# Expert routing: the weight blocks' low halves go from GpSimd to VectorE, a third pair of weight tiles, one staging copy per four tokens

## The chip, the cores and the metric

One core of one Trainium2 chip runs the whole kernel. The metric is the device time of one execution in microseconds, of which a lower one is better; the time shown is the median of several executions of the compiled program. One further execution is recorded by the hardware profiler, and all rows below come from it.

## The reference

The kernel computes two network blocks on 512 tokens of width 1024, all in fp32. The change lies in the first block, in its layer of product-key experts (PEER). Cut to what matters here:

```python
PEER_HEADS, PEER_NKEYS, PEER_TOPK = 8, 128, 16        # 128 x 128 experts
def block(xb):                                        # xb: 128 tokens x 1024
    q = (xb @ w_query).reshape(T, PEER_HEADS, 2, PEER_HALF)
    s = jnp.einsum('thpk,hpnk->thpn', q, sub_keys)
    top_s, top_i = lax.top_k(s, PEER_TOPK)
    cand_s = top_s[:, :, 0, :, None] + top_s[:, :, 1, None, :]
    cand_i = top_i[:, :, 0, :, None] * PEER_NKEYS + top_i[:, :, 1, None, :]
    best_s, best_pos = lax.top_k(cand_s.reshape(...), PEER_TOPK)
    idx = jnp.take_along_axis(cand_i.reshape(...), best_pos, axis=-1)
    gate = jax.nn.softmax(best_s, axis=-1)
    act = jax.nn.gelu(jnp.einsum('td,thkd->thk', xb, expert_u[idx]), approximate=False)
    return jnp.einsum('thk,thkd->td', gate * act, expert_v[idx])
```

Each token uses 8 x 16 = 128 of 16384 experts.

## The kernel before

The 512 tokens are four groups of 128. Group 0 is done sparsely: for each of its 128 slots an indirect DMA on GpSimd's queue gathers one row of `u` per token (later one of `v`), and VectorE takes the dot product with `hT0` (L712). This is the generator `sparse`; `y0["ahead"]` says how many gathers are issued ahead of the dot product that uses them. Groups 1 to 3 (384 tokens) are done densely: TensorE multiplies the tokens with all 16384 rows of `u`, in 128 blocks of 128 experts, and a matrix `Wd` of gates (expert by token, zero where an expert wasn't chosen) masks the result.

Every fp32 weight tile is used as two halves: `whi`, a cast to the matmul's fp32r made by ScalarE, and `wlo`, the difference, made by the engine in `lo_eng[0]` (`split`, L261 to L263). A block (`ublock`, L663) is 24 products of 128x384 in eight k-steps of three, followed by a Gelu on ScalarE into `ge`, which is stored to `gd` in HBM. 76 (`AHEAD`) of the 128 blocks are done during the routing, between other work, and the rest in the loop over experts behind it, whose first product writes `py` (L1002).

The routing runs as follows.

- `gemm_cm("w_q", ...)` with `cons_q` (L735) makes the queries and scores. ScalarE copies the query tile to `qc` (L737), and VectorE finds the 16 best keys of each half (the last row of that is L748).
- `route(t)` (L783) makes, for group t, the 16 best of the candidates, their indices (`eq`, L814, a comparison of 128x800) and the gates, on VectorE. For t = 0 that ends in `idx0`, which the gathers need. For t > 0 `pk` (gates and the two index halves, last cast L836) is transposed on TensorE (L841) and copied to `pT`. `route` yields seven times inside its heads and then a few times more.
- `scatter(t)` (L850) builds `Wd` for group t. Per token it needs a one-hot `ao` (128x128, row index times gate) and a one-hot `bo`, whose product on TensorE (L879) is the token's 128x128 gate matrix. VectorE makes four tokens' `bo` in one operation (L856) and most `ao` (L868), ScalarE makes some `ao` in two steps (`ab` L865, `ao` L866). ScalarE copies the products, four tokens at a time, to `stg` (L881). A scatter yields 16 times, each time after 8 tokens.
- The driver (L891) calls `lookahead(nb, ns)` at each yield: `nb` blocks (or half a block in a scatter), some stores of `Wd`, and `ns` steps of the sparse group. It runs route 0, route 1, scatter 1, route 2, scatter 2, route 3, scatter 3, and then the blocks that are left up to 76.

`lookahead` keeps five raw tiles loading ahead (`us`, `uload`) and splits the next two blocks (`usplit`). The raw tiles and the gather targets come from rings set by `set_ring`, the halves from the pool `whl` with two buffers each. Before, the routing runs with:

```python
        lo_eng[0] = G
            y0 = {"ahead": 5}
            gemm_cm("w_q", range(16), 8, ah, al, cons_q, cols=128, late=LATE[1])
                        if w == 3 and u % 8 == 0:
        lo_eng[0] = V
```

so that GpSimd makes every `wlo` from the query product to the end of the routing. The order of instructions on each engine is decided by a scheduler at build time from the program's order and its dependencies, and each engine runs its own row in that order.

Of the kernel before, what the change touches and what calls it, by code (L numbers as in the profile page):

```python
# [8 lines left out]
F32 = mybir.dt.float32  # L9
F32R = mybir.dt.float32r  # L10
# [171 lines left out]
def build(tc, A, out):  # L182
    nc = tc.nc
    V, S, G, PE = nc.vector, nc.scalar, nc.gpsimd, nc.tensor
    with ExitStack() as ctx:
# [5 lines left out]
        def rpool(name, bufs=1):  # L191
            return pool(name, bufs, side="right")
# [17 lines left out]
        whl = body.enter_context(pool("whl", 2))  # L210
# [13 lines left out]
        def set_ring(w=2048, **n):  # L224

            rawx.close()
            ring.update(w=w, i={}, n={}, p={})
            grow_ring(**n)
# [36 lines left out]
        lo_eng = [G]  # L265
# [42 lines left out]
        def gemm_cm(*a, **k):  # L308
            for _ in gemm_gen(*a, **k):
                pass  # L310
# [132 lines left out]
        with rpool("hg") as hg:  # L443
# [15 lines left out]
            with rpool("hgl") as hl_:  # L459
                lmask = hl_.tile([128, 7, 128], F32)  # L460
                nc.scalar.dma_start(lmask, A["cst"][:, 3:])
                q = hl_.tile([128, 4, T], F32)
# [156 lines left out]
        rawx.close()  # L619
        gp = peer.enter_context(pool("gp"))  # L620
        AHEAD = 76
        set_ring(1024, raw=6, g=5)
        set_banks(pg=2, ps=6)
        hT0 = gp.tile([128, D], F32)
        gate0 = gp.tile([128, 128], F32)
# [23 lines left out]
        Wd = dr.tile([128, 128, ND], F32)  # L649
        gd = dr.tile([AHEAD, 128, ND], F32)  # L650

        def uload(b):
            raw = rawtile((8, 128))
            nc.sync.dma_start(raw.rearrange("p k c -> p (k c)"), A["uT"][b])
            return raw

        def usplit(raw):
            hi = whl.tile([128, 8, 128], F32R, name="whi")
            lo = whl.tile([128, 8, 128], F32R, name="wlo")
            split(raw, hi, lo, lo_eng[0])  # L660
            return hi, lo

# [63 lines left out]
        lo_eng[0] = G  # L726
        with ExitStack() as rt0, ExitStack() as rt_:
            rt = rt0.enter_context(rpool("rt"))
            rk = rt_.enter_context(rpool("rk"))
            keys = rk.tile([128, 16, 128], F32)  # L730
            nc.sync.dma_start(keys, A["keysT"])
# [15 lines left out]
                    V.max(ts[t][:, n, 8:], s2)  # L747
                    V.max_index(ti[t][:, n, 8:], ts[t][:, n, 8:], s2)  # L748

            y0 = {"ahead": 5}  # L750

            rest = sparse(y0)
            nu = [0, 0.0]
            pend = []
# [23 lines left out]
                    nu[1] -= 1  # L778

            gemm_cm("w_q", range(16), 8, ah, al, cons_q, cols=128, late=LATE[1])  # L780
            rt_.close()
            rs = rt_.enter_context(rpool("rs"))

            def route(t):
# [49 lines left out]
                V.tensor_scalar(ii[:, 1], ii[:, 0], 127, None, op0=OP.bitwise_and)  # L834
                V.tensor_scalar(ii[:, 0], ii[:, 0], 7, None, op0=OP.logical_shift_right)
                V.tensor_copy(pk[:, 1:3], ii)  # L836
                yield
                yield
                pp = psum()
                for a in range(3):  # L840
                    PE.transpose(pp[:, a * 128:(a + 1) * 128], pk[:, a], ident)  # L841
# [7 lines left out]
            def scatter(t):  # L849

                pT, nT = tr[t]
                stg = [rs.tile([128, 32, 128], F32, name=f"stg{q}") for q in range(4)]

                def onehots(u):
                    bo = rs.tile([128, 4, 128], F32, name="bo", bufs=3)
                    V.tensor_tensor(bo, iota[:, None, :].to_broadcast([128, 4, 128]),  # L856
                                    pT[:, 1, u:u + 4, None].to_broadcast([128, 4, 128]), op=OP.is_equal)
                    aos = []
                    for w in range(4):
                        tk = u + w  # L860
                        ao = rs.tile([128, 128], F32, name="ao", bufs=8)
                        if w == 3 and u % 8 == 0:

                            ab = rt.tile([128, 128], F32, name="ab", bufs=2)
                            S.activation(ab, iota, AF.Abs, bias=nT[:, 1, tk:tk + 1])  # L865
                            S.activation(ao, ab, AF.Relu, scale=nT[:, 0, tk:tk + 1], bias=pT[:, 0, tk:tk + 1])  # L866
                        else:
                            V.tensor_scalar(ao, iota, pT[:, 2, tk:tk + 1], pT[:, 0, tk:tk + 1], op0=OP.is_equal, op1=OP.mult)  # L868
                        aos.append(ao)
                    return bo, aos  # L870

                oh = [onehots(0)]
                for u in range(0, 128, 4):
                    if u < 124:
                        oh.append(onehots(u + 4))
                    bo, aos = oh.pop(0)
                    pw = psum()
                    for w in range(4):
                        PE.matmul(pw[:, w * 128:(w + 1) * 128], aos[w], bo[:, w], start=True, stop=True)  # L879
                    for q in range(4):  # L880
                        S.copy(stg[q][:, :, u:u + 4].rearrange("p i t -> p t i"),  # L881
                               pw.rearrange("p (t i) -> p t i", t=4)[:, :, q * 32:(q + 1) * 32])
                    if u % 8 == 4:
                        yield
                for q in range(4):
                    for i in range(0, 32, 4):
                        pend.append((Wd[q * 32 + i:q * 32 + i + 4, :, t * 128 - 128:t * 128].rearrange("i p t -> p i t"),
                                     stg[q][:, i:i + 4]))

            tr = {}  # L890
            for t in range(2):  # L891
# [12 lines left out]
            for _ in range(y0["ahead"] - 1):  # L904
                y0["ahead"] -= 1
                next(rest)
        lo_eng[0] = V

        yx = peer.enter_context(rpool("yx"))
        dg = yx.tile([128, 4, 128], F32)  # L910
# [51 lines left out]
        with rpool("ex") as ex:  # L962
# [45 lines left out]
            w = (256 - y0["i"]) / (AHEAD + (LAST - AHEAD) * 3)  # L1008
# [39 lines left out]
            for n in range(2):  # L1048
                raw = rawtile((8, 128))
                nc.sync.dma_start(raw, A["w_in2"][0].rearrange("p (k c) -> p k c", k=8)[:, :, n * 128:n * 128 + 128])  # L1050
                first[n] = whalf(raw, 8, 0, 128)
            q = finish([1, 2, 3], py)
# [418 lines left out]
        with rpool("sd") as sd:  # L1471
# [25 lines left out]
            u = d32("u")  # L1497
# [217 lines left out]
        for d in range(2):  # L1715
            pos_ = [psum("po") for _ in range(4)]
            for j in range(4):
                raw = rawtile((2, 512))
                nc.sync.dma_start(raw.rearrange("p k c -> p (k c)"), A["w_out2"][d * 4 + j])
                hi = whl.tile([128, 2, 512], F32R, name="whi")  # L1720
                lo = whl.tile([128, 2, 512], F32R, name="wlo")
# [27 lines left out]
        ahead = {}  # L1749
# [31 lines left out]
        q = rsqrt(vv, 4)  # L1781
# [213 lines left out]
        for p in range(16):  # L1995
            o, q = divmod(p, 2)
# [108 lines left out]
```

## Time and profile before

| what | value |
|---|---|
| time, median of 3 executions | 3310.78 us (3307.57 to 3311.12) |
| the profiled execution's own time | 3308.83 us |
| its span in the trace | 3307.1 us |
| mean granted clock of TensorE | 0.977 |
| TensorE busy | 3110.3 us, 94% |
| VectorE busy | 2199.8 us, 67% |
| ScalarE busy | 1122.1 us, 34% |
| GpSimd busy | 816.2 us, 25% |
| `wlo` on GpSimd (L263), whole kernel | 120 operations, 306.6 us |
| `wlo` on VectorE (L263), whole kernel | 190 operations, 220.2 us |

Busy time is the time in which an instruction of that engine runs; a matmul's end is modelled, and an instruction of VectorE that is held up inside counts as busy. The span leaves out what lies around the recorded work, here 1.7 us. PE is TensorE, DVE VectorE, ACT ScalarE, POOL GpSimd, SP the queue that issues plain DMAs.

### The profile page before, as it was taken

Reading aid. Unit: us, or ns where it says so; the run is one execution under the profiler, and the core shown is the slowest. Engines: PE = TensorE matmul, PEld = TensorE weight load, DVE = VectorE, ACT = ScalarE, POOL = GpSimd, SP = SyncE. Lnnn points to the kernel's source line nnn. Section 1 sums busy time; section 2 is a strip of 40 time slices with the busy share of each in tenths; the row PEclk is TensorE's granted clock in tenths of the full one; section 3 lists DMA queues with packets and bytes.
Section 4 is the critical chain, followed back from the end, with each engine's and each line's share of the span. In section 5 each row is a group of like instructions: output and inputs, shape, how many; then the busy total and the mean of one; then the engine's idle time right before and its main releaser. Section 6 shows DMA issues by size and latency. Waiting matters only on the chain. (4 is left out here: it accounts for less than half of the span.)

```text
span 3307.1 us, 54224 instructions
## 1 busy us (share of the span) xinstructions
PE 3110.3 (94%) x21581; PEld 2423.5 (73%) x21581; DVE 2199.8 (67%) x4329; ACT 1122.1 (34%) x2012; POOL 816.2 (25%) x495
## 2 busy tenths in 40 slices
PE   7999996878999999999989999999999988999997
PEld 4877786878988888999977777777777756444443
DVE  5834689997828887888976767676568763232323
ACT  3222332645633333333333323332265532111111
POOL 2221244354344444555510000000001151000000
PEclk9999998989999999999999999999999988999999
DMA  5243335375599999999932222222364346899995
GB/s 201 73 182 115 134 104 163 122 245 181 168 345 375 369 368 328 353 358 359 355 109 103 71 73 75 75 75 69 102 248 155 131 154 242 366 403 403 394 412 222
DMA packets 234707, 725.85 MB, mean 219 GB/s; under 512 B 21904, under 2 KB 110736, under 8 KB 197456
## 3 DMA queue, kind: packets, MB, share of 16 engines
q1 hardware_dynamic: 187312, 567.64, 46.5%
q0 software_dynamic: 36864, 134.23, 11.2%
q10 hardware_dynamic: 10272, 20.45, 1.7%
q8 instruction: 171, 2.80, 0.3%
q14 instruction: 88, 0.72, 0.1%
HBM read 658.93 MB, written 63.31 MB: 218 GB/s over the span
## 5 line engine op out<-in xcount | busy, mean ns | idle before, releaser
L262 ACT CAST whi<-raw 128x1024 fp32r<-128x1024 f32 (+1 forms) x310 | 310.8, 1003 | 715.6 <-PE pg L292 384.2
L263 POOL TENSOR_TENSOR wlo<-raw,whi 128x1024 fp32r<-128x1024 f32 x120 | 306.6, 2557 | 550.9 <-ACT whi L262 475.0
L291 PE MATMUL pg<-ah,whi 128*128 128x512 f32 x1056 | 427.3, 405 | 3.5 <-DVE th L1435 2.8
L292 PE MATMUL pg<-al,whi 128*128 128x512 f32 x1056 | 424.2, 402 | 1.7 <-DVE al L263 1.7
L293 PE MATMUL pg<-ah,wlo 128*128 128x512 f32 x1056 | 422.7, 401 | 1.7 <-POOL wlo L263 1.6
L670 PE MATMUL pg<-ah,wlo 128*128 128x384 f32 x1024 | 349.6, 341 | 37.9 <-POOL wlo L263 34.5
L670 PE MATMUL pg<-ah,whi 128*128 128x384 f32 x1024 | 352.9, 345 | 2.3 <-ACT ge L672 1.8
L670 PE MATMUL pg<-al,whi 128*128 128x384 f32 x1024 | 348.0, 340 | 0.0
L263 DVE TENSOR_TENSOR wlo<-raw,whi 128x1024 fp32r<-128x1024 f32 (+1 forms) x190 | 220.2, 1160 | 190.1 <-ACT whi L262 187.2
L1002 PE MATMUL py<-vh,gh 128*128 128x512 f32 x768 | 299.5, 390 | 2.3 <-ACT ge L672 2.3
L1004 PE MATMUL py<-vh,gl 128*128 128x512 f32 x768 | 300.6, 391 | 0.0
L1003 PE MATMUL py<-vl,gh 128*128 128x512 f32 x768 | 300.4, 391 | 0.0
L700 POOL DMA_INDIRECT g<-in_u_dram,idx x128 | 196.2, 1533 | 268.1 <-DVE g L712 221.1
L291 PEld LDWEIGHTS pg<-ah,whi 128*128 128x128 f32 x1056 | 199.9, 189 | 52.1 <-issue 5.9
L293 PEld LDWEIGHTS pg<-ah,wlo 128*128 128x128 f32 x1056 | 200.2, 190 | 46.8 <-POOL wlo L263 2.4
L292 PEld LDWEIGHTS pg<-al,whi 128*128 128x128 f32 x1056 | 200.2, 190 | 44.4 <-issue 3.6
L670 PEld LDWEIGHTS pg<-ah,wlo 128*128 128x128 f32 x1024 | 196.7, 192 | 41.7 <-POOL wlo L263 38.0
L700 POOL DMA_INDIRECT g<-in_v_dram,idx x128 | 189.0, 1477 | 135.5 <-DVE y L720 100.4
L670 PEld LDWEIGHTS pg<-ah,whi 128*128 128x128 f32 x1024 | 196.8, 192 | 4.9 <-ACT ge L672 2.1
L1894 PE MATMUL pf<-we,XT 128*64 128x512 f32 x720 | 197.9, 596 | 2.3 <-ACT XT L1980 2.3
L670 PEld LDWEIGHTS pg<-al,whi 128*128 128x128 f32 x1024 | 196.4, 192 | 2.1
L1946 DVE TENSOR_TENSOR mrg<-mrg,pc 128x512 f32<-128x512 f32 x128 | 84.5, 684 | 139.7 <-PE pc L1944 139.7
(658 smaller groups left out, 6010.3 us busy)
## 6 DMA issues: line engine op xcount, KB each, us to landing
raw<-in_uT_dram SPq DMA_DIRECT2D x128, 512.0 KB
raw<-in_v_dram SPq DMA_DIRECT2D x128, 512.0 KB
raw<-in_w_in_dram SPq DMA_DIRECT2D x54, 1024.0 KB
we<-in_we_down_dram SPq DMA_DIRECT2D x47, 1024.0 KB
we<-in_we_up_dram SPq DMA_DIRECT2D x46, 1024.0 KB
we<-in_we_gate_dram SPq DMA_DIRECT2D x44, 1024.0 KB
araw<-in_w_ada_dram SPq DMA_DIRECT2D x24, 1024.0 KB
Wd<-stg SPq DMA_DIRECT2D x96, 256.0 KB
```

Source lines behind the costliest of these rows:

```text
L262: S.copy(dst_hi, src)
L263: (eng or V).tensor_sub(dst_lo, src, dst_hi.bitcast(F32))
L291: a = PE.matmul(ps, l_ix(lh, k), r_ix(rh, k), start=k == 0, stop=False)
L292: a = PE.matmul(ps, l_ix(lh, k), r_ix(rl, k), start=False, stop=False)
L293: a = PE.matmul(ps, l_ix(ll, k), r_ix(rh, k), start=False, stop=k == kc - 1)
L670: PE.matmul(ps[:, :ND], w[:, k], a[:, k, 128:], start=k + n == 0, stop=k + n == 9)
L700: G.indirect_dma_start(out=raw, out_offset=None, in_=u if i < 128 else v, in_offset=bass.IndirectOffsetOnAxis(ap=idx0[:, k:k + 1], axis=0))
L1002: PE.matmul(py[t][d], gh[:, tk], vh[:, dsl], start=b == 0, stop=False)
L1003: PE.matmul(py[t][d], gh[:, tk], vl[:, dsl], start=False, stop=False)
L1004: PE.matmul(py[t][d], gl[:, tk], vh[:, dsl], start=False, stop=b == 127)
L1894: PE.matmul(pp[e * CAP:(e + 1) * CAP], xg(hf * 4 + k, e), ws[e][k], start=hf + k == 0, stop=hf == 1 and k == 3)
L1946: V.tensor_add(xo, xo, po)
```

## The change

From the end of the query product on, VectorE makes `wlo` instead of GpSimd, whose queue then holds only the gathers. A third pair of `whi` and `wlo` tiles, in the pool `whx`, is used by every third block while the routing lasts; the raw ring has five tiles instead of six and the gather ring four instead of five, and three gathers are issued ahead instead of five. The staging tile of a scatter is one tile instead of four, written by one copy of 128x512 per four tokens instead of four of 128x128. ScalarE makes the fourth `ao` of every four tokens, instead of every second four. `route(t)` for t > 0 yields three times behind its last cast instead of twice, so that one block more lies in each. After the change the lines are numbered 6 to 10 higher.

```diff
--- before.py
+++ after.py
@@ -619,7 +619,7 @@
         rawx.close()
         gp = peer.enter_context(pool("gp"))
         AHEAD = 76
-        set_ring(1024, raw=6, g=5)
+        set_ring(1024, raw=5, g=4)
         set_banks(pg=2, ps=6)
         hT0 = gp.tile([128, D], F32)
         gate0 = gp.tile([128, 128], F32)
@@ -654,9 +654,16 @@
             nc.sync.dma_start(raw.rearrange("p k c -> p (k c)"), A["uT"][b])
             return raw
 
+        whx = []
+
         def usplit(raw):
-            hi = whl.tile([128, 8, 128], F32R, name="whi")
-            lo = whl.tile([128, 8, 128], F32R, name="wlo")
+            p = whl
+            if whx:
+
+                p = whx[0] if whx[1] % 3 == 2 else whl
+                whx[1] += 1
+            hi = p.tile([128, 8, 128], F32R, name="whi")
+            lo = p.tile([128, 8, 128], F32R, name="wlo")
             split(raw, hi, lo, lo_eng[0])
             return hi, lo
 
@@ -726,6 +733,7 @@
         lo_eng[0] = G
         with ExitStack() as rt0, ExitStack() as rt_:
             rt = rt0.enter_context(rpool("rt"))
+            whx += [rt0.enter_context(rpool("whx")), 0]
             rk = rt_.enter_context(rpool("rk"))
             keys = rk.tile([128, 16, 128], F32)
             nc.sync.dma_start(keys, A["keysT"])
@@ -747,7 +755,7 @@
                     V.max(ts[t][:, n, 8:], s2)
                     V.max_index(ti[t][:, n, 8:], ts[t][:, n, 8:], s2)
 
-            y0 = {"ahead": 5}
+            y0 = {"ahead": 3}
 
             rest = sparse(y0)
             nu = [0, 0.0]
@@ -778,6 +786,8 @@
                     nu[1] -= 1
 
             gemm_cm("w_q", range(16), 8, ah, al, cons_q, cols=128, late=LATE[1])
+
+            lo_eng[0] = V
             rt_.close()
             rs = rt_.enter_context(rpool("rs"))
 
@@ -834,8 +844,8 @@
                 V.tensor_scalar(ii[:, 1], ii[:, 0], 127, None, op0=OP.bitwise_and)
                 V.tensor_scalar(ii[:, 0], ii[:, 0], 7, None, op0=OP.logical_shift_right)
                 V.tensor_copy(pk[:, 1:3], ii)
-                yield
-                yield
+                for _ in range(3):
+                    yield
                 pp = psum()
                 for a in range(3):
                     PE.transpose(pp[:, a * 128:(a + 1) * 128], pk[:, a], ident)
@@ -849,7 +859,7 @@
             def scatter(t):
 
                 pT, nT = tr[t]
-                stg = [rs.tile([128, 32, 128], F32, name=f"stg{q}") for q in range(4)]
+                stg = rs.tile([128, 128, 128], F32, name="stg")
 
                 def onehots(u):
                     bo = rs.tile([128, 4, 128], F32, name="bo", bufs=3)
@@ -859,7 +869,7 @@
                     for w in range(4):
                         tk = u + w
                         ao = rs.tile([128, 128], F32, name="ao", bufs=8)
-                        if w == 3 and u % 8 == 0:
+                        if w == 3:
 
                             ab = rt.tile([128, 128], F32, name="ab", bufs=2)
                             S.activation(ab, iota, AF.Abs, bias=nT[:, 1, tk:tk + 1])
@@ -877,15 +887,11 @@
                     pw = psum()
                     for w in range(4):
                         PE.matmul(pw[:, w * 128:(w + 1) * 128], aos[w], bo[:, w], start=True, stop=True)
-                    for q in range(4):
-                        S.copy(stg[q][:, :, u:u + 4].rearrange("p i t -> p t i"),
-                               pw.rearrange("p (t i) -> p t i", t=4)[:, :, q * 32:(q + 1) * 32])
+                    S.copy(stg[:, :, u:u + 4].rearrange("p i t -> p t i"), pw.rearrange("p (t i) -> p t i", t=4))
                     if u % 8 == 4:
                         yield
-                for q in range(4):
-                    for i in range(0, 32, 4):
-                        pend.append((Wd[q * 32 + i:q * 32 + i + 4, :, t * 128 - 128:t * 128].rearrange("i p t -> p i t"),
-                                     stg[q][:, i:i + 4]))
+                for i in range(0, 128, 4):
+                    pend.append((Wd[i:i + 4, :, t * 128 - 128:t * 128].rearrange("i p t -> p i t"), stg[:, i:i + 4]))
 
             tr = {}
             for t in range(2):
@@ -904,7 +910,7 @@
             for _ in range(y0["ahead"] - 1):
                 y0["ahead"] -= 1
                 next(rest)
-        lo_eng[0] = V
+        whx.clear()
 
         yx = peer.enter_context(rpool("yx"))
         dg = yx.tile([128, 4, 128], F32)
```

The first place is VectorE's row in scatter 3, just behind the operation that ends route 3 (`nT`, L845). `bo` and `ao` are the one-hots. Before, they stand there alone:

```order
L845 TENSOR_SCALAR nT<-pT 128x256
L856 TENSOR_TENSOR bo<-cst,pT 128x512
L868 TENSOR_SCALAR ao<-cst,pT 128x128 x3
L856 TENSOR_TENSOR bo<-cst,pT 128x512
L868 TENSOR_SCALAR ao<-cst,pT 128x128 x4
L856 TENSOR_TENSOR bo<-cst,pT 128x512
L868 TENSOR_SCALAR ao<-cst,pT 128x128 x3
L856 TENSOR_TENSOR bo<-cst,pT 128x512
L868 TENSOR_SCALAR ao<-cst,pT 128x128 x4
```

In the changed program the same place reads:

```order
L866 TENSOR_TENSOR bo<-cst,pT 128x512
L878 TENSOR_SCALAR ao<-cst,pT 128x128 x3
L263 TENSOR_TENSOR wlo<-raw_7096,whi 128x1024
L878 TENSOR_SCALAR ao<-cst,pT 128x128 x3
L866 TENSOR_TENSOR bo<-cst,pT 128x512
L878 TENSOR_SCALAR ao<-cst,pT 128x128 x3
L866 TENSOR_TENSOR bo<-cst,pT 128x512
L878 TENSOR_SCALAR ao<-cst,pT 128x128 x3
L866 TENSOR_TENSOR bo<-cst,pT 128x512
L263 TENSOR_TENSOR wlo<-raw_7138,whi 128x1024
L878 TENSOR_SCALAR ao<-cst,pT 128x128 x3
```

There are three `ao` of every four tokens now, and one `wlo` for about every four `bo`.

The second place is GpSimd's row where the routing goes from A to the first scatter; `g` is a gather's target, `idx` holds `idx0`. Before:

```order
L263 TENSOR_TENSOR wlo<-raw_5359,whi 128x1024
L263 TENSOR_TENSOR wlo<-raw_5401,whi 128x1024
L263 TENSOR_TENSOR wlo<-raw_5444,whi 128x1024
L700 DMA g_7680<-in_u_dram,idx_2289 128x1024
L700 DMA g_7911<-in_u_dram,idx_2289 128x1024
L700 DMA g_8130<-in_u_dram,idx_2289 128x1024
L263 TENSOR_TENSOR wlo<-raw_5486,whi 128x1024
L700 DMA g_8209<-in_u_dram,idx_2289 128x1024
L700 DMA g_8288<-in_u_dram,idx_2289 128x1024
```

In the changed program the whole stretch of the routing reads like this:

```order
L707 DMA g_6002<-in_u_dram,idx_2289 128x1024
L707 DMA g_6217<-in_u_dram,idx_2289 128x1024
L707 DMA g_6432<-in_u_dram,idx_2289 128x1024
L707 DMA g_6635<-in_u_dram,idx_2289 128x1024
L707 DMA g_7397<-in_u_dram,idx_2289 128x1024
L707 DMA g_7612<-in_u_dram,idx_2289 128x1024
L707 DMA g_7827<-in_u_dram,idx_2289 128x1024
L707 DMA g_8030<-in_u_dram,idx_2289 128x1024
```

No `wlo` is left between the gathers, so that a gather waits only for `idx0` and a free target.

The third place is ScalarE's row in scatter 3, with the casts (`whi`), the Gelu (`ge`), the copies (`stg`) and the one-hots (`ab`, `ao`). Before:

```order
L881 COPY stg_7205<-ps 128x4x32
L881 COPY stg_7206<-ps 128x4x32
L881 COPY stg_7207<-ps 128x4x32
L881 COPY stg_7208<-ps 128x4x32
L262 CAST whi<-raw_7723 128x1024
L672 ACTIVATE ge<-pg 128x384
L881 COPY stg_7205<-ps 128x4x32
L881 COPY stg_7206<-ps 128x4x32
L881 COPY stg_7207<-ps 128x4x32
L881 COPY stg_7208<-ps 128x4x32
L866 ACTIVATE ao<-ab,pT,nT 128x128
```

In the changed program:

```order
L262 CAST whi<-raw_7542 128x1024
L679 ACTIVATE ge<-pg 128x384
L890 COPY stg<-ps 128x4x128
L876 ACTIVATE ao<-ab,pT,nT 128x128
L890 COPY stg<-ps 128x4x128
L875 ACTIVATE ab<-cst,nT 128x128
L876 ACTIVATE ao<-ab,pT,nT 128x128
L875 ACTIVATE ab<-cst,nT 128x128
L890 COPY stg<-ps 128x4x128
L876 ACTIVATE ao<-ab,pT,nT 128x128
L890 COPY stg<-ps 128x4x128
L876 ACTIVATE ao<-ab,pT,nT 128x128
```

Four copies became one, and between two casts there are now four pairs `ab` and `ao`, not two.

## Rows read from the trace of the kernel before

**Rows 1.** Stretches A to T: us; PE, PEld, DVE, ACT, POOL busy; PEclk, DMA share, GB/s.

```profile
463.20:574.00 110.80, 82.75 (x445) 80.66 (x444) 109.47 (x336) 34.47 (x47) 55.72 (x27) 0.88 0.49 159
574.00:648.50 74.50, 65.59 (x435) 62.88 (x435) 73.96 (x190) 52.76 (x173) 26.36 (x10) 0.97 0.29 91
648.50:717.30 68.80, 47.92 (x258) 46.31 (x257) 68.80 (x146) 18.39 (x30) 42.78 (x22) 0.88 0.94 297
717.30:793.60 76.30, 67.28 (x437) 64.50 (x437) 75.25 (x160) 51.11 (x171) 23.92 (x8) 0.95 0.29 98
793.60:841.50 47.90, 46.13 (x257) 45.48 (x256) 12.71 (x20) 16.73 (x28) 30.70 (x15) 0.96 1.05 335
841.50:905.80 64.30, 62.35 (x437) 61.15 (x437) 63.83 (x142) 49.29 (x170) 20.02 (x8) 1.00 0.35 122
905.80:970.70 64.90, 61.43 (x352) 60.18 (x350) 10.43 (x11) 25.05 (x39) 35.61 (x17) 1.00 1.02 329
```

**Rows 2.** Timeline of GpSimd: start, duration, engine, line, operation, wait before it.

```profile
730.64 2.95 POOL L263 TENSOR_TENSOR wlo<-raw,whi 128x1024 fp32r<-128x1024 f32 x1 [9.39 <-ACT whi L262]
738.39 3.71 POOL L263 TENSOR_TENSOR wlo<-raw,whi 128x1024 fp32r<-128x1024 f32 x1 [4.80 <-ACT whi L262]
...
913.34 2.38 POOL L263 TENSOR_TENSOR wlo<-raw,whi 128x1024 fp32r<-128x1024 f32 x1 [1.78 <-ACT whi L262]
917.50 2.38 POOL L263 TENSOR_TENSOR wlo<-raw,whi 128x1024 fp32r<-128x1024 f32 x1 [1.77 <-ACT whi L262]
```

**Rows 3.** Waits of TensorE from 463.2 to 970.7: total us, times, longest.

```profile
PE pg L670 <- POOL wlo L263: 34.5, 10, 14.0
PE ps L879 <- DVE ao L868: 23.6, 20, 4.4
```

**Rows 4.** Timeline of VectorE in S1; x4 is four operations taken together.

```profile
581.64 1.11 DVE L868 TENSOR_SCALAR ao<-cst,pT 128x128 f32<-128x128 f32 x4
582.67 0.68 DVE L856 TENSOR_TENSOR bo<-cst,pT 128x512 f32<-128x512 f32 x1
583.27 2.94 DVE L868 TENSOR_SCALAR ao<-cst,pT 128x128 f32<-128x128 f32 x3
```

**Rows 5.** Timeline of GpSimd beside it.

```profile
583.67 2.46 POOL L263 TENSOR_TENSOR wlo<-raw,whi 128x1024 fp32r<-128x1024 f32 x1 [6.41 <-ACT whi L262]
```

**Rows 6.** Groups of VectorE in S1, then in R2: count, busy us, mean ns.

```profile
L868 DVE TENSOR_SCALAR ao<-cst,pT 128x128 f32<-128x128 f32 x109 | 45.8, 479 | 0.5 <-PE ps L879 0.5
...
L712 DVE SCALAR_TENSOR_TENSOR g<-g,hT 128x1024 f32<-128x1024 f32 x12 | 24.0, 1997 | 0.0
L814 DVE TENSOR_TENSOR eq<-bpf,cst 128x800 f32<-128x800 f32 x8 | 7.9, 983 | 0.0
L868 DVE TENSOR_SCALAR ao<-cst,pT 128x128 f32<-128x128 f32 x2 | 0.6, 334 | 0.0
```

**Rows 7.** Timeline of VectorE and of GpSimd in S1, around a gather.

```profile
598.56 1.22 DVE L712 SCALAR_TENSOR_TENSOR g<-g,hT 128x1024 f32<-128x1024 f32 x1
...
599.70 0.87 DVE L868 TENSOR_SCALAR ao<-cst,pT 128x128 f32<-128x128 f32 x3
...
600.06 0.95 POOL L700 DMA_INDIRECT g<-in_u_dram,idx  x1 [5.57 <-DVE ao L868]
```

**Rows 8.** A group of VectorE in A.

```profile
L814 DVE TENSOR_TENSOR eq<-bpf,cst 128x800 f32<-128x800 f32 x16 | 23.6, 1476 | 0.0
```

**Rows 9.** Groups of ScalarE in S3: count, busy us, mean ns.

```profile
L881 ACT COPY stg<-ps 128x128 f32<-128x128 f32 x124 | 33.4, 431 | 10.9 <-PE ps L879 10.9
L262 ACT CAST whi<-raw 128x1024 fp32r<-128x1024 f32 x8 | 8.4, 1044 | 4.1 <-issue 4.1
L866 ACT ACTIVATE ao<-ab,pT,nT 128x128 f32<-128x128 f32 x16 | 7.8, 485 | 0.0
```

**Rows 10.** ScalarE's copies `qc` in the query product: shortest/median/longest ns.

```profile
L737 ACT COPY qc<-pg x16: 575/575/581, 369.4 to 464.2; 128x512 f32<-128x512 f32 x16
```

**Rows 11.** Waits of SP's DMA queue from 990 to 1280 us, in the expert loop.

```profile
SPq L968 <- DVE vl L263: 119.9, 61, 3.0
```

## The prediction

> **What bounds the kernel now.** I read the busy table cut at the stages of the routing first, then the waits of TensorE, then the rows of VectorE, GpSimd and ScalarE. The stretch that the change touches runs from 463.2 to 970.7 us. I call its seven pieces, in the order of the rows, A (routing of token groups 0 and 1), S1, R2, S2, R3, S3 (scatter and routing of groups 1 to 3 by turns) and T (the expert blocks left over) [rows 1]. The reader is to see that VectorE is busy throughout A, S1, R2, S2 and S3 and nearly idle in R3 and T. TensorE, which must do 76 blocks of the hidden layer in any case, is not: it idles, and its granted clock has a mean of 0.88 in A and R2, the two pieces where it idles most, so part of them ran at the lower of its levels (1.2 against 2.4 GHz).
>
> How much is lost: a block alone takes 4.16 us (in T the low halves of one block and the next start at 913.34 and 917.50), and in a scatter a block with its 16 one-hot products takes 7.75 us where nothing is late (730.64 to 738.39) [rows 2]. Now 38 blocks lie in A, R2 and R3, 24 in the scatters, 14 in T: 52 x 4.16 + 24 x 7.75 = 402 us. The stretch takes 507.5, so about 105 us are waits and slow clock. Of the waits 34.5 us are for `wlo` from GpSimd, 23.6 us for `ao` from VectorE [rows 3]. The longest of them, 14.0 us, lies in A, where GpSimd's queue holds gathers, which need VectorE's `idx0`, ahead of the next `wlo`.
>
> **Why VectorE is full.** Its busy time is partly waiting. Four `ao` at 581.64 are followed 1.03 us later by a `bo`, and that 0.60 us later by three more `ao` [rows 4]: an `ao` left alone is 0.257 us of VectorE's time, a `bo` 0.60. But those three take 2.94 us, because GpSimd makes a `wlo` from 583.67 on [rows 5]; left alone, three take 0.87 (599.70) [rows 7], so 2.1 us are lost. The mean `ao` of S1 is 479 ns, one left alone 334 ns by itself: 109 x 0.145 = 15.8 us lost to 8 `wlo` [rows 6], and S2 loses about as much. In R2 twelve dot products (L712) average 1997 ns against 1.22 us for the one at 598.56, left alone: 9.3 us [rows 6, 7]. Summed over all groups of R2 in the same way I get 21.4 us. In A the sixteen operations of L814 average 1476 ns where R2 has 983: 7.9 us [rows 6, 8], with the other groups 27. So each `wlo` on GpSimd costs VectorE 1.6 to 2.4 us, and TensorE waits for VectorE.
>
> **The change, part by part.** *The subtraction on VectorE.* The 190 that VectorE makes elsewhere average 1.16 us (the table of the profile before); the dot product of the same size at 598.56 lets the next operation start after 1.14 [rows 7], which I take. It removes the stall of 1.6 to 2.4. GpSimd keeps only gathers, and these do not stall VectorE: at 599.70 three `ao` take 0.87 us with a gather at 600.06 in their middle [rows 7].
>
> *A.* VectorE is busy 109.5 of the 110.8 us [rows 1]. Less 25 of stalls (2 fall into the query product's end), plus 18 `wlo` x 1.14 = 20.5 by the order: 4.5 us less. I take 6, since VectorE no longer starts with work left over from a stalled query product. Its new order has no `wlo` for some 24 us in the middle of A, so TensorE still idles there, and A stays bound by VectorE. 110.8 becomes **104.5**, with one block more done in its idle time (19).
>
> *S1, S2, S3.* A block costs VectorE 4 x 0.60 + 12 x 0.257 + 1.14 = 6.6 us now (four `ao` of 16 go to ScalarE, not two), below TensorE's 7.75; before, 4 x 0.60 + 14 x 0.257 + 2.1 = 8.1, above it. So TensorE binds: 8 x 7.75 = 62, with 1 to 1.5 for the start **63.5, 63.5 and 63** against 74.5, 76.3 and 64.3.
>
> *The copies and `ab`/`ao` on ScalarE.* Sixteen copies a block at 33.4 / 124 = 0.27 us [rows 9] become four of 128x512; such a copy takes 0.575 us for `qc` [rows 10], where the target is contiguous. Bounds: 4 x 0.575 = 2.3 us a block, or no gain, 4.3. I take 2.3: the small copies wrote the same stride. ScalarE is busy 49.3 us for the 8 blocks of S3 [rows 1], 6.2 each; less 2.0, plus two pairs `ab`, `ao` at 0.485 an operation [rows 9], 1.9: 6.1, or 8.1 by the other bound, which is above TensorE's 7.75 by 0.4, 3 us a scatter. By the order each `ao` of ScalarE stands a half-block ahead of its product, so no wait is added.
>
> *R2.* VectorE's 68.8 us lose 21.4 of stalls and seven of the twelve dot products, which the new order puts elsewhere (7 x 1.14 = 8), and gain 12 `wlo` (13.7): 53, less 2 for other rows that moved, 51. VectorE begins it some 3 us before TensorE ends S1, and the first one-hots need 1.5: **49.5**. TensorE's own 11 blocks need 45.8.
>
> *R3.* 11 blocks instead of 10, 45.8 us, and 2 for DMA (rival 1): **48** against 47.9. *T.* 11 blocks instead of 14, 45.8, and 5 for DMA and for the turn to the expert loop: **51** against 64.9.
>
> *Third pair, rings.* A block's `whi` and `wlo` wait for the block three back, not two, so the cast can be done when VectorE comes to its `wlo`: covered. With one raw tile less the load is still issued five blocks ahead. Price if not: one 512 KB load at 335 GB/s [rows 1], 1.6 us, now and then.
>
> *Gathers.* `ahead` 3 and fewer turns of the last loop leave 4 of 256 gathers more to the expert loop: 2.1 MB. There SP waits 119.9 us for VectorE to free raw tiles [rows 11], so DMA runs ahead of use: 0, at most 2.1 MB / 335 GB/s = 6 us if it does not. The loop begins with less loaded, since T is shorter: I take 3 us, bounds 0 and 10.
>
> Sum: 104.5 + 63.5 + 49.5 + 63.5 + 48 + 63 + 51 = 443 against 507.5, -64.5, and +3: **-61.5 us**. From the profiled execution's 3308.8 us that is 3247; its time lies 2 us below the median of the runs, so, rounded, **3250 us**.
>
> **A rule against it.** By the row at 599.70 gathers cost VectorE nothing [rows 7]. The Trainium skill, "SBUF — State Buffer", section "Who interferes with whom", says that VectorE and GpSimd share one pair of ports, which an `ao` in a two-port mode and a gather's descriptors would lock against each other: whichever starts first blocks the other wholly. By the row the sum stays; by the rule each gather in the routes and scatters has a price, and rival 3 is the outcome.
>
> **Rivals.**
> 1. *DMA takes the saving back.* R2, R3 and T ran at 297, 335 and 329 GB/s with the DMA share at 0.94 to 1.05 [rows 1]: 20.4, 16.0 and 21.4 MB. A gather is 0.52 MB, a block 0.72 (load and `gd`). After: R2 seven gathers less, one block more, 17.5 MB; R3 one block and three gathers more, 18.3; T three blocks less, 19.2. At those three rates 59, 55 and 58 us, 9.5 + 7 + 7 = 23 above mine: **3273**. For it: shares at 1. Against it: R3 ran blocks at near their own pace at this load, and stores may end in the next scatter, which uses 91 to 122 GB/s.
> 2. *TensorE binds everywhere but in A:* R2 46, R3 46, T 48, nothing at the loop's start: **3238**.
> 3. *Gathers stall VectorE:* some 12 of them in A and R2, where VectorE binds, each for its own 0.95 us [rows 7]: 11 us, **3261**. The row at 599.70 speaks against it.
> 4. *Slower: VectorE stands in line behind ScalarE.* Now `wlo` waits in VectorE's queue for the cast, the cast behind ScalarE's copies, the copies for TensorE's products, and the next `ao` behind `wlo`. If the one-hots kept ahead (three `bo`, eight `ao`) did not cover that, a scatter block would add copy 0.6 [rows 10], cast 1.04 [rows 9] and `wlo` 1.2 to 7.75: 10.6 us, 85 a scatter, 64 in all: **3314**. It decides from about 2.6 us more a scatter block (61.5 / 24). Against it: by the order the cast stands some 3 us ahead of the one-hots behind it.
> 5. *No change:* the routing's own chain (top-16, indices, transposes) holds A and R2 at their length (25 us), VectorE's rows around the transposes hold the scatters at theirs (25, what S1, S2 and S3 were to give), and DMA keeps T at 60 (rival 1: 7): 57 lost of 61.5, **3307**.
>
> **How the numbers follow.** My forecast 0.62, rivals in turn 0.18, 0.07, 0.04, 0.05, 0.04. The range 3232 to 3284 reaches from rival 2, with 6 us for a better A, to rival 1 with the loop's 10 us; rivals 4 and 5 stay out. A difference of 0.2% (6.6 us) is about what a measurement of this kernel can tell. Faster: 0.62 + 0.18 + 0.07 + 0.04 = 0.91; same 0.04; slower 0.05.
>
> **What would show it.** Right: no `wlo` on GpSimd in the stretch, mean `ao` near 0.33 us and L712 near 1.2; in the scatters a block each 7.8 us and VectorE with idle time; TensorE at clock 1.00 from S1 on, its waits left in A; the expert loop's first product near 910 us, not 970.7. Wrong: waits of the blocks for `whi` or raw loads (rival 1), `ao` still long beside gathers (3), scatter blocks above 8.5 us with VectorE waiting for ScalarE's `whi` (4).

## The result and the profile after

The changed kernel takes 3251.06 us (median of 5, 3249.2 to 3252.64) against 3310.78 us (median of 5, 3306.46 to 3314.47) for the kernel before, measured beside it. The ratio is 0.9821, 95% interval 0.981 to 0.9832. The forecast was 3250 us, range 3232 to 3284. The total hides errors of both signs, which the stages show.

Below is the table of busy time of the changed kernel, cut at the same events as [rows 1]: the end of the query product's first part (463.2 us in both), the first and the last one-hot product of each scatter, and the first `py` product. The columns are those of [rows 1].

```profile
463.20:566.00 102.80, 87.43 (x478) 85.53 (x476) 100.57 (x333) 36.48 (x48) 8.74 (x8) 0.92 0.52 173
566.00:626.40 60.40, 59.64 (x431) 58.98 (x431) 59.81 (x194) 59.68 (x110) 1.88 (x2) 1.00 0.33 102
626.40:678.10 51.70, 48.36 (x281) 48.03 (x279) 51.70 (x147) 22.21 (x33) 5.20 (x4) 1.00 1.02 327
678.10:741.40 63.30, 62.76 (x437) 61.85 (x438) 61.20 (x146) 60.97 (x110) 0.00 (x0) 0.97 0.35 122
741.40:797.50 56.10, 50.91 (x281) 49.39 (x279) 38.00 (x52) 18.46 (x28) 13.69 (x9) 0.97 1.06 365
797.50:859.70 62.20, 61.96 (x438) 61.80 (x439) 52.70 (x134) 59.98 (x109) 0.00 (x0) 0.97 0.34 112
859.70:914.80 55.10, 47.97 (x277) 47.65 (x275) 13.84 (x13) 17.90 (x26) 3.76 (x4) 0.97 1.02 325
```

| stretch | before | forecast | after |
|---|---|---|---|
| A | 110.8 | 104.5 | 102.8 |
| S1 | 74.5 | 63.5 | 60.4 |
| R2 | 68.8 | 49.5 | 51.7 |
| S2 | 76.3 | 63.5 | 63.3 |
| R3 | 47.9 | 48 | 56.1 |
| S3 | 64.3 | 63 | 62.2 |
| T | 64.9 | 51 | 55.1 |
| sum | 507.5 | 443 | 451.6 |

The first `py` product starts at 914.75 us instead of 970.7, 56.0 us earlier; the span is 59.6 us shorter. The other 3.6 us lie near the end of the expert loop and behind it, where nothing was changed: the two profiles stand 55.7 us apart at the 601st `py<-vh,gh` product and 58.5 at the last. In the profiles of all kernels of this study that part varies by some microseconds. I therefore compare profiles at a point inside the loop as well (a table stands behind the experiments).

TensorE's columns, summed over the seven stretches, split the 56 us: its idle time falls from 74.1 to 32.6 us, and its busy time for the same work (2621 and 2623 instructions) from 433.5 to 419.0, while the granted clock rises from 0.88 to 0.92 in A and from 0.88 to 1.00 in R2.

VectorE's groups in A, S1 and R2 of the changed kernel, by form (count, busy us, mean ns), answer to [rows 6, 8]:

```profile
L824 DVE TENSOR_TENSOR eq<-bpf,cst 128x800 f32<-128x800 f32 x16 | 15.8, 987 | 0.0
...
L878 DVE TENSOR_SCALAR ao<-cst,pT 128x128 f32<-128x128 f32 x95 | 27.2, 346 | 0.6 <-PE ps L889 0.6
L263 DVE TENSOR_TENSOR wlo<-raw,whi 128x1024 fp32r<-128x1024 f32 x8 | 9.8, 1220 | 0.0
...
L719 DVE SCALAR_TENSOR_TENSOR g<-g,hT 128x1024 f32<-128x1024 f32 x4 | 4.9, 1215 | 0.0
```

The same operations run close to the durations they had when left alone: `ao` 346 ns (479 before, 334 alone), L719 1215 ns (1997 before), the comparisons of A 987 (1476 before, 983 alone). The low half costs VectorE 1.22 us. What TensorE waits for, from 463.2 to 914.9 us, answers to [rows 3]:

```profile
PE pg L677 <- DVE wlo L263: 13.4, 2, 11.7
PE py L1008 <- ACT ge L679: 7.1, 1, 7.1
PE ps L889 <- DVE ao L878: 6.2, 4, 3.3
PE pg L677 <- ACT ge L679: 4.7, 5, 1.9
```

The waits for low halves fell from 34.5 to 13.4 us, those for `ao` from 23.6 to 6.2. Two long waits are left: 11.7 us for a low half in A, and 7.1 us in T, in front of the first `py` product.

### The profile page after: what moved, and what is told of

It is laid out like the page before. It is cut to its first block, busy times and chain, and to the rows that moved or that the text cites. A ratio compares the mean times of both kernels' runs of the same rounds, so it can differ in the third digit from the quotient of the medians.

```text
span 3247.5 us, 53973 instructions
## 1 busy us (share of the span) xinstructions
PE 3093.4 (95%) x21581; PEld 2412.3 (74%) x21581; DVE 2175.1 (67%) x4357; ACT 1152.4 (35%) x1820; POOL 621.2 (19%) x419
## 5 line engine op out<-in xcount | busy, mean ns | idle before, releaser
L263 DVE TENSOR_TENSOR wlo<-raw,whi 128x1024 fp32r<-128x1024 f32 (+1 forms) x266 | 312.9, 1177 | 233.4 <-ACT whi L262 224.1
L293 PEld LDWEIGHTS pg<-ah,wlo 128*128 128x128 f32 x1056 | 199.7, 189 | 48.3 <-POOL wlo L263 4.0
L263 POOL TENSOR_TENSOR wlo<-raw,whi 128x1024 fp32r<-128x1024 f32 x44 | 110.6, 2517 | 335.4 <-ACT whi L262 271.7
```

What stands on the lines that cost most here:

```text
L263: (eng or V).tensor_sub(dst_lo, src, dst_hi.bitcast(F32))
L293: a = PE.matmul(ps, l_ix(ll, k), r_ix(rh, k), start=False, stop=k == kc - 1)
```

## The experiments

Two theories were set against each other. *Hold-up:* a GpSimd subtraction holds VectorE's own instructions up, and that was the loss. *Late results:* the loss was that TensorE waited for `wlo`, which GpSimd makes slowly, behind gathers, into one of only two pairs. Beside them stood the question of which of the parts bring the gain.

**The subtraction alone.** The kernel before with one line:

```diff
             gemm_cm("w_q", range(16), 8, ah, al, cons_q, cols=128, late=LATE[1])
+            lo_eng[0] = V
```

> The kernel before, with one edit: VectorE makes the low halves from the end of the query product on; two pairs of weight tiles, four copies, the old share of the one-hots, two turns behind the last cast. If the gain is GpSimd's subtraction no longer holding VectorE up, this alone brings most of it: a scatter block costs VectorE 4 x 0.60 + 14 x 0.257 + 1.14 = 7.1 us, under TensorE's 7.75, so about -48 us, near 3262. If the third pair is needed, because a low half in VectorE's queue waits for a cast that waits for a pair to come free, at most half of it comes, 3285 or more, with waits of VectorE for the cast in the scatters.

3251.26 us, ratio 0.982 (0.98 to 0.984): the whole gain, more than either expectation. The sum of its stretches is that of the changed kernel within 3 us, but the stretches are not: R3 takes 66.0 us and T 63.2, R2 47.0 and S3 55.8, since its blocks lie elsewhere. In its S1 the `ao` are short again:

```profile
L869 DVE TENSOR_SCALAR ao<-cst,pT 128x128 f32<-128x128 f32 x111 | 31.3, 343 | 0.7 <-PE ps L880 0.7
L857 DVE TENSOR_TENSOR bo<-cst,pT 128x512 f32<-128x512 f32 x31 | 21.3, 687 | 0.0
L263 DVE TENSOR_TENSOR wlo<-raw,whi 128x1024 fp32r<-128x1024 f32 x7 | 8.5, 1221 | 0.8 <-ACT whi L262 0.8
```

With two pairs VectorE waited 0.8 us there for a cast. The third pair is not needed for it.

**All but the subtraction.** The changed kernel with

```diff
-            lo_eng[0] = V
             rt_.close()
...
         whx.clear()
+        lo_eng[0] = V
```

> The changed kernel with GpSimd making the low halves as before: third pair, one copy, fourth one-hot on ScalarE, three turns stay. If the stalls were the loss, VectorE's scatter block is 4 x 0.60 + 12 x 0.257 + 2.1 = 7.6 instead of 8.1 us, so the scatters gain at most 0.5 x 24 = 12 us and the routes nothing: 3297 to 3308. If it was GpSimd's late low halves (a pair that came free late), the third pair mends that, and the time falls to about 3280.

3304.3 us, ratio 0.9979 (0.997 to 0.9989): faster by 0.2%, inside the first expectation. The third pair and all the other parts together are worth no more than that while GpSimd subtracts: S1 takes 76.6 us, and its `ao` are long:

```profile
L877 DVE TENSOR_SCALAR ao<-cst,pT 128x128 f32<-128x128 f32 x92 | 40.7, 494 | 2.2 <-PE ps L888 2.2
...
L263 POOL TENSOR_TENSOR wlo<-raw,whi 128x1024 fp32r<-128x1024 f32 x8 | 27.8, 3476 | 57.0 <-ACT whi L262 57.0
```

**An extra GpSimd subtraction that no product waits for.** The changed kernel with

```diff
             split(raw, hi, lo, lo_eng[0])
+            if whx and lo_eng[0] is V:
+                G.tensor_sub(raw, raw, hi.bitcast(F32))
             return hi, lo
```

> The changed kernel, and for each block of the routing GpSimd also subtracts the high half from the raw tile into the raw tile itself, which nothing but the next load into it waits for. If a GpSimd subtraction holds VectorE up, some 2 us of stall come back per block wherever VectorE binds (A, S1, R2, part of the others): mean one-hot near 0.48 us again in the scatters, and 25 to 45 us more than the changed kernel, 3276 to 3296. If the loss was that TensorE waited for GpSimd's results and for its queue, nothing of that comes back: 3251 to 3257, one-hots near 0.33 us.

3352.62 us, ratio 1.0128 (1.0106 to 1.0149): 101.6 us above the changed kernel, far more than expected, and slower than the kernel before. A takes 140.3 us, with VectorE busy 139.9 of them. Rows of VectorE in A, of GpSimd in A, and of VectorE in S1:

```profile
L721 DVE SCALAR_TENSOR_TENSOR g<-g,hT 128x1024 f32<-128x1024 f32 x4 | 13.0, 3250 | 0.0
...
L669 POOL TENSOR_TENSOR raw<-raw,whi 128x1024 f32<-128x1024 f32 x19 | 54.7, 2883 | 49.6 <-DVE wlo L263 48.2 <-issue 1.4
...
L880 DVE TENSOR_SCALAR ao<-cst,pT 128x128 f32<-128x128 f32 x92 | 40.5, 494 | 0.0
```

The one-hot is back at 494 ns and the dot product at 3250, so hold-up is shown with no product waiting for GpSimd's result. ScalarE's casts do wait for the subtraction, which reads `whi` (25.8 us in A), but VectorE's own waits in A are 0.2 us in all, so that did not make A long. My range was wrong because I had added the stall only where the kernel before was bound by VectorE. Here VectorE carries its own subtraction too: 19 x 2 us = 38 on the 102.8 of A is 141, and a scatter block costs 6.6 + 2.1 = 8.7 us, 70 a scatter (measured 72.6, 74.1 and 69.9).

**A GpSimd operation that only writes.** As above, with `G.memset(raw, 0.0)` instead.

> As the run with the extra subtraction, but GpSimd only fills the dead raw tile with zeros: it writes and reads nothing. If any GpSimd operation on the tiles holds VectorE up, it is as slow as the one with the subtraction, per microsecond of GpSimd work; if it is GpSimd's reading that does it, it costs nothing, 3251 to 3255, with the 128x800 comparisons at 0.9 us and one-hots near 0.33.

3260.4 us, ratio 0.9855 (0.9834 to 0.9875): 9 us above the changed kernel by the medians, between the expectations. Groups of VectorE and of GpSimd in S1, then three `ao` beside a memset, three alone, and that memset:

```profile
L880 DVE TENSOR_SCALAR ao<-cst,pT 128x128 f32<-128x128 f32 x95 | 30.7, 430 | 0.1
...
L669 POOL MEMSET raw<- 128x1024 f32 x8 | 8.2, 1030 | 48.4 <-DVE wlo L263 43.3 <-issue 5.1
```

```profile
584.86 1.38 DVE L880 TENSOR_SCALAR ao<-cst,pT 128x128 f32<-128x128 f32 x3
...
586.75 0.85 DVE L880 TENSOR_SCALAR ao<-cst,pT 128x128 f32<-128x128 f32 x3
...
585.05 1.04 POOL L669 MEMSET raw<- 128x1024 f32 x1 [6.28 <-DVE wlo L263]
```

Writing holds up `ao`, which has one tensor input: three take 1.38 us beside a memset and 0.85 without, so 0.5 us is lost for each memset, about 4 us over the eight of S1, which took 64.7 us instead of 60.4. (The mean of 430 ns says more than that, since two `ao` that wait at the same time both count the wait.) What has two tensor inputs is seen at the first `bo` of scatter 2, which in both runs begins just after an operation of GpSimd has begun. With the extra subtraction, then with the memset:

```profile
748.35 2.85 DVE L868 TENSOR_TENSOR bo<-cst,pT 128x512 f32<-128x512 f32 x1
...
748.31 2.35 POOL L669 TENSOR_TENSOR raw<-raw,whi 128x1024 f32<-128x1024 f32 x1 [0.40 <-DVE wlo L263]
```

```profile
683.38 0.68 DVE L868 TENSOR_TENSOR bo<-cst,pT 128x512 f32<-128x512 f32 x1
...
683.36 0.98 POOL L669 MEMSET raw<- 128x1024 f32 x1 [0.43 <-issue]
```

The subtraction, which also reads, holds it up, and the memset does not. The comparisons of A, at 984 ns here, can't tell: all that overlap a memset began before it or in its last 0.12 us. That splits the mechanism by the kind of operation. The Trainium skill, "SBUF — State Buffer", section "Who interferes with whom", says the same: a VectorE operation with two inputs in SBUF contends with GpSimd's reads and not with its writes, one with a single input contends when it runs in a two-port mode; the trace agrees by these rows.

**No third pair.** The changed kernel with

```diff
-                p = whx[0] if whx[1] % 3 == 2 else whl
+                p = whx[0] if False else whl
```

> The changed kernel without the third pair of weight tiles. The subtraction alone gave the whole gain with two pairs, so the third pair should be worth nothing: 3251, within 4 us. If it hides the cast from VectorE's queue, as the prediction had it, taking it away shows waits of VectorE for the cast in the scatters and 5 us or more, 3256 to 3270.

3248.88 us, ratio 0.9814 (0.9794 to 0.9835): no difference. VectorE's waits for the cast are 1.0 us in S1 and 0.7 in S2.

**Four copies.** The changed kernel with

```diff
-                    S.copy(stg[:, :, u:u + 4]..., pw.rearrange("p (t i) -> p t i", t=4))
+                    for q in range(4):
+                        S.copy(stg[:, q * 32:(q + 1) * 32, u:u + 4]..., pw...[:, :, q * 32:(q + 1) * 32])
```

> The changed kernel with four copies of 128x128 into the staging tile per four tokens. With four pairs of one-hot operations a block ScalarE then needs 8.1 us a block by the prediction's bound, over TensorE's 7.75: 3 us a scatter, 3260, if the one copy is what saved ScalarE 2 us a block. If the one copy brought no time, 3251.

3252.56 us, ratio 0.9831 (0.9811 to 0.9852): no difference, and the two groups say why. ScalarE in S3 with one copy, then, in the second block, with four:

```profile
L890 ACT COPY stg<-ps 128x512 f32<-128x512 f32 x31 | 33.6, 1085 | 1.9 <-PE ps L889 1.9
L876 ACT ACTIVATE ao<-ab,pT,nT 128x128 f32<-128x128 f32 x32 | 15.7, 490 | 0.0
```

```profile
L891 ACT COPY stg<-ps 128x128 f32<-128x128 f32 x124 | 33.7, 439 | 0.8 <-PE ps L889 0.7
```

33.6 us for 31 copies, 33.7 for 124: the same work.

**The old share of the one-hots.** The changed kernel with `if w == 3 and u % 8 == 0:` again.

> The changed kernel with ScalarE making the fourth one-hot of every second four tokens only. VectorE's scatter block is then 7.1 us instead of 6.6. If TensorE binds the scatters, no difference, 3251. If VectorE, busy 59.8 of 60.4 us in the first scatter, binds that one, 16 x 0.257 = 4 us there, 3255. If the trade cost something (ScalarE is busy 59.7 of 60.4 us there too), it is faster, 3247.

3254.63 us, ratio 0.9843 (0.9824 to 0.9862). The interval overlaps that of the changed kernel. The medians stand 3.6 us apart, but the scatters themselves are not longer (59.5, 62.1, 60.0), so VectorE did not bind S1, and no gain of this part is shown.

**Two turns.** The changed kernel with the two `yield` of before.

> The changed kernel with two turns behind the last cast of a route, so three blocks fewer lie in the routes and three more in T. The blocks cost TensorE 4.16 us wherever they lie; routes 2 and 3 and T all run at a DMA share near 1, so moving a block moves its 0.72 MB with it: 3251, within 4 us. If the third turn filled idle time of TensorE in A and route 2, taking it away costs 4 to 8 us: 3255 to 3259.

3255.66 us, ratio 0.9841 (0.9824 to 0.9857), at the edge of the second expectation by the medians. The profile does not bear it out: R2 is 46.4, R3 52.8 and T 61.1, and its first `py` product, at 915.18, stands where that of the changed kernel does. Undecided within 4 us.

**Light loads.** The changed kernel, with 64 KB loaded instead of 512 for blocks 47 to 61, which leaves most of these experts' weights out:

```diff
+            if 47 <= b < 62:
+                nc.sync.dma_start(raw[:, 0], A["uT"][b][:, :128])
+                return raw[:, 0:1].to_broadcast([128, 8, 128])
             nc.sync.dma_start(raw.rearrange("p k c -> p (k c)"), A["uT"][b])
```

> The changed kernel, but blocks 47 to 61 load one k-step of their weights instead of eight, and use it eight times (part of the experts' weights is left out). All engines do the same work; route 3, which takes 56.1 us for some 11.5 blocks at a DMA share of 1.06, moves 15 x 0.46 = 6.9 MB less. If DMA binds it, as rival 1 said, it falls to TensorE's 48 to 50 us, about 6 us less, 3245. If route 3 is long for another cause (the one-hots of scatter 3 or VectorE), it stays, 3251.

3240.33 us, ratio 0.9802 (0.978 to 0.9824). Its R3:

```profile
738.10:788.40 50.30, 48.62 (x281) 47.89 (x279) 38.03 (x52) 18.40 (x28) 13.70 (x9) 1.00 1.01 327
```

5.8 us less than the 56.1, with no other work taken away: so the loads held a part of R3. ScalarE's waits for raw loads there in the changed kernel, and in this one:

```profile
ACT whi L262 <- DMA raw<-in_uT_dram: 22.8, 6, 6.9
```

```profile
ACT whi L262 <- DMA raw<-in_uT_dram: 16.8, 5, 5.5
```

The DMA share is still 1.01, since 32 stores of `Wd` of 256 KB each run there as well. A was 3 us shorter in this run too, for no reason that its edit gives, so not all of the 10.7 us between the medians is the loads'; by the ratios, whose intervals overlap, it is 6 us.

**Turns among the best candidates.** VectorE's order in A has no `wlo` for some 24 us, while route 1 finds its best candidates, and TensorE waits 11.7 us there. The changed kernel with

```diff
                     V.max_index(bp[:, h, 8:], bs[:, h, 8:], c2)
+                    if t < 2 and h in (2, 5):
+                        yield
```

> The changed kernel with two more turns in the loop over the heads' best candidates (after heads 2 and 5) in routes 0 and 1, so that VectorE's order has low halves in the 24 us of A that had none, where TensorE waited 11.7 us. Four blocks more lie in A and four fewer in T. If the order of VectorE makes that wait, it is gone: A grows by 4 x 1.14 us of VectorE less than that, T shrinks from 55 us by up to 4 x 0.72 MB at 325 GB/s = 9 us. Since the expert loop's start then has less loaded, I expect a part back: 3246, 3241 to 3251.

3239.9 us, ratio 0.9788 (0.9772 to 0.9804), 11 us better than the changed kernel and just below the expected range. TensorE's waits for low halves in the whole stretch, then A and T:

```profile
PE pg L677 <- DVE wlo L263: 3.4, 2, 1.7
```

```profile
463.20:572.00 108.80, 103.44 (x575) 101.38 (x574) 107.14 (x345) 42.40 (x58) 9.28 (x8) 0.97 0.56 192
...
863.10:900.90 37.80, 31.26 (x181) 30.94 (x179) 7.28 (x8) 11.31 (x17) 3.58 (x4) 0.95 1.02 320
```

TensorE is busy 103.4 of A's 108.8 us, and T gives back 17 us for the 6 that A grew.

**The same with 80 blocks ahead** (`AHEAD = 80`).

> As the run with the four turns more in A, and 80 blocks done ahead instead of 76, so that T keeps its 11 blocks and the expert loop has four blocks' hidden layer fewer to do: 4 x 4.16 = 16.6 us of TensorE out of the loop, where TensorE is busy throughout, against some 5 us more in A: about 3239. If the loop is bound by DMA instead, those blocks save it 4 x (512 - 192) KB, 3.5 us: 3251.

3237.9 us, ratio 0.9789 (0.9773 to 0.9806). The first expectation, about 3239, fits, but against the run with 76 no gain of the four blocks is shown.

**Only the subtraction, the turns and 80 blocks**, on the kernel before: the edits of the first run and of the last two together.

> The kernel before with the subtraction on VectorE, the four turns among the best candidates of routes 0 and 1, and 80 blocks ahead; none of the other parts of the change (two pairs, rings and four copies as before, the old share of the one-hots, two turns behind the last cast). If those parts bring nothing, as the subtraction alone said, it is as fast as the changed kernel with the same turns: 3238, within 4 us. If the third pair or the lighter VectorE block pays once A is dense, it is slower, 3243 to 3250.

3241.53 us, ratio 0.9789 (0.9775 to 0.9803). The time is inside the first expectation, and the ratio is that of the changed kernel with the same turns, so the other parts are worth nothing there either.

The profiles at a point inside the expert loop, where all have settled (start of the 49th `py<-vh,gh` product; the runs with 80 blocks differ from there on and are left out):

| kernel | first `py` product, us | 49th, us | behind the changed kernel at the 49th |
|---|---|---|---|
| before | 970.70 | 1005.09 | +55.7 |
| changed | 914.75 | 949.38 | 0 |
| subtraction alone | 917.3 | 951.7 | +2.3 |
| all but the subtraction | 968.41 | 1003.99 | +54.6 |
| extra subtraction | 1015.25 | 1050.19 | +100.8 |
| memset | 920.34 | 954.48 | +5.1 |
| no third pair | 908.47 | 947.38 | -2.0 |
| four copies | 915.59 | 949.88 | +0.5 |
| old share of one-hots | 915.57 | 949.68 | +0.3 |
| two turns | 915.18 | 947.95 | -1.4 |
| light loads | 902.36 | 937.79 | -11.6 |
| turns in A, 76 | 900.88 | 937.71 | -11.7 |

## Why the prediction was right, and where it was not

**VectorE held up by GpSimd: right, and now shown.** The extra subtraction brings the long one-hots back with no product waiting for its result, and the lone one-line edit brings the whole gain. How much of the 56 us came from TensorE no longer waiting for GpSimd's late results, beside the hold-up, no run separates. Rivals 4 and 5 are out: scatter blocks take 60.4 / 8 to 63.3 / 8, 7.6 to 7.9 us, as forecast, and VectorE's waits for a cast are 2.0 us in A and none in the scatters. Two signs were missed: the granted clock was to be 1.00 from S1 on, and is 0.97 in S2, R3, S3 and T, and VectorE was to have idle time in the scatters, but has only 0.6 us in S1.

**Gathers cost nothing: right.** With gathers alone on GpSimd the groups shown above run close to their own pace. Rival 3 is out, and so is rival 2, since R3 and T took 56 and 55 us. The Trainium skill's "SBUF — State Buffer", section "Who interferes with whom", would have let a gather's descriptors and `ao` lock each other; a gather at 615.33 in S1 of the changed kernel shows nothing of it, and the memset does. Only two of the stretch's 27 gathers run beside `ao`, so the test is a small one.

```profile
614.96 0.88 DVE L878 TENSOR_SCALAR ao<-cst,pT 128x128 f32<-128x128 f32 x3
...
615.33 0.94 POOL L707 DMA_INDIRECT g<-in_u_dram,idx  x1 [70.23 <-DVE ao L878]
```

**A, and the hole in it: right.** 102.8 against 104.5, with 11.7 us of TensorE's idle time where VectorE's order has no `wlo`. The turns took that wait away, and all that they do is to move blocks into that place, so the order was its cause.

**R3 and T: mis-sized.** The step "45.8 us, and 2 for DMA: 48" gave R3 8 us too little, and T was 4 too low. Rival 1's division of bytes by rate gave 55 and 58 for them, against 56.1 and 55.1, but 59 for R2, which took 51.7. Its mechanism was right for R3, its agreement in part luck: it had 18.3 MB at 335 GB/s, and R3 moved 20.5 MB at 365, with nine gathers instead of the five of before. The light loads put 5.8 us of R3 down to transfers, by one profile. The run with all but the subtraction has the same 11 blocks, loads and stores in its R3 and no gather: 15.9 MB, TensorE busy throughout, and the forecast length.

```profile
802.90:851.20 48.30, 48.30 (x280) 47.95 (x278) 2.74 (x4) 18.22 (x28) 26.46 (x11) 1.00 1.05 329
```

So both terms were too small. TensorE's own work is 48.3 us by that row, not 45.8, since half a block more lies in R3 (some 276 block products, 24 a block, 11.5 blocks). And the "2 for DMA", with the gathers that the new order puts beside R3's loads and stores, is about 8: TensorE waits 5.1 us there and is busy 50.9 instead of 48.3 at a granted clock of 0.97. Of the waits 2.4 us stand in front of the first one-hots of scatter 3, where I had put a term into R2 and none into R3; with light loads they are 0.6. T's excess is a wait for a load too. The 7.1 us in front of the first `py` product are put down to the Gelu `ge`, which stands in ScalarE's order behind a cast that waits for a load of `v`:

```profile
913.26 1.04 ACT L262 CAST vh<-raw 128x1024 fp32r<-128x1024 f32 x1 [4.46 <-DMA raw<-in_v_dram]
914.21 0.48 ACT L679 ACTIVATE ge<-pg 128x384 f32<-128x384 f32 x1
```

**The loop's start: hidden.** I took +3 us; the first 48 `py<-vh,gh` products take 34.6 us against 34.4 before, so nothing was lost beyond the 7.1 us wait already in T. The run without a third pair shows the coupling: its T was 5.6 us shorter, and the first 48 products took 38.9 us instead of 34.6. I read T and the loop's start as one budget of transfers.

**The other parts: right to cost nothing, wrong to help.** The copy was sized wrong: I took 0.575 us, from a contiguous target, where it is 1.085, the bound of "no gain". ScalarE was therefore busy 60 us in S3, 7.5 a block, just under TensorE's 7.75, and the miss cost nothing. The lighter VectorE block (6.6 instead of 7.1 us) and the third pair bought slack that nothing used.

That the total agreed so well is luck in part. The routing gave 56.0 us instead of 64.5; the 3 us that I took off for the loop's start were not lost, and the end of the kernel gave 3.6 that I had not forecast and that no run explains. From the start of the last `py<-vh,gh` product to the end of the span the profiles of these kernels show 1585.5 to 1591.4 us for the same work, so differences of that size need not be this change's, and I leave it open.

## What to carry to other kernels

When an engine is busy all the time, compare the mean of its operations with the same form left alone, before taking its busy share for its work: here each GpSimd subtraction took 1.6 to 2.4 us of VectorE's time, and moving the operation to the engine that it held up cost that engine 1.22 us and saved it more. Then take the edits apart on the chip: one line carried this change. Look also for stretches in an engine's order in which one kind of instruction is missing, since a few turns placed there were worth 11 us more.

## What the runs showed of the hardware

- A GpSimd `memset` of 128x1024 (1.03 us) holds up `tensor_scalar` with one tensor input (three in 1.38 us, 0.85 without it) and not `tensor_tensor` with two (`bo` 0.68 us beside it); a GpSimd subtraction holds up both, by about 2 us (`bo` 2.85 us); an indirect gather holds up neither (27 gathers, two of them beside `ao`).
- The rows suggest that it works both ways: GpSimd's own subtraction takes 2.38 us in T, where VectorE is nearly idle, and 2.95 and 3.71 us in S2, where it is busy [rows 2].
- A ScalarE copy of 128x512 from PSUM takes 0.575 us into contiguous SBUF [rows 10] and 1.085 us into a tile with 512 bytes from one element to the next; four copies of 128x128 with that stride take the same 1.08 us in all. The Trainium skill, "SBUF — State Buffer", section "Door 1: The DMA port swizzle", says that accesses which leave a 16-byte line each time pay a penalty; the trace agrees, and shows that a longer instruction does not take it away.
